# Second-layer modulation vectors: from TensorE steps to weighted sums on VectorE

## The chip, the core and the metric

The kernel runs on one core of one Trainium2 chip. The metric is the device time of one execution in microseconds. The kernel before takes 1640.04 us, the median of three runs (1639.86 to 1642.47).

## What is computed

Two blocks follow each other on 256 tokens of width 1024. The first block has two layers: a hybrid layer (sliding-window attention beside a chunked delta rule), then a recurrent one, each with a squared-ReLU MLP of hidden width 4096. The second block has two layers with two streams, the 256 tokens and 256 context tokens. Its layer 0 works on both streams; its layer 1, the last, needs of the context only keys and values, and its MLP has one stream. Each layer of the second block is steered by modulation vectors: for both of two conditioning vectors it needs six vectors of 1024,

```
m = silu(c) @ w_mod[i] + b_mod[i]        # c: (1024,), w_mod[i]: (1024, 6 * 1024)
shift1, scale1, gate1, shift2, scale2, gate2 = split(m, 6)
h  = rmsnorm(x, g) * (1 + scale1) + shift1
```

The two conditioning vectors (one for the tokens, one for the context) are known from the start, so the vectors of both layers can be computed at any time before they are used. The weights w_mod are 2 x 25 MB in fp32, of 259.77 MB that the kernel moves in all.

## The kernel before

**Numbers.** Large products run on TensorE as three products of fp32r pairs: each weight unit (1 MB, tile `wr`) is split by `w_split` (L395) into a high part `wh`, a cast on ScalarE (L407), and a rest `wl`, a difference on VectorE (L408). Four such pairs of 1024 columns are kept, two raw units. `w_next` (L424) loads the next unit and splits one half ahead.

**Order.** The program is written out as Python generators that are woven. At build time a planner orders the instructions of each engine: an instruction's rank is its place in the program, and of those whose inputs and buffers are there in the planner's own model the one of lowest rank goes first. `tc.high_priority(-10)` gives ranks ten places later. The engines then work through fixed orders, and an instruction that waits holds the ones behind it on its engine. So a step may run long before the place where it is written, where its engine has a pause, its tiles are there and a buffer is free; at its place it is due.

**The steps.** `mods` (L749) is a generator of 48 steps, 24 for each of the second block's layers i: three pairs q of vectors, eight pieces k of 128 rows each. A step needs two tiles `wm` of 128 x 1024 (512 KB each, four buffers, loaded by `mod_load`, L728). It makes four matmuls of the conditioning columns `cs_t[:, k]` (128 x 32) with 512 columns of weights each, into four bands of 32 output partitions of the bank `pm`, and sums over k there. After the eighth, bias and gain (`bg`) are applied on VectorE, the gates go to DRAM (`mdr`), and `cols_of` transposes shift and scale into the columns `mc`.

**Where the steps are written.** `fill(n)` takes n steps. 18 are in `some_mods` (L1204), woven with the delta rule and the attention of the hybrid layer, one in every second round; two after it (L1219); four in each MLP of one stream in the first block (L614) and two after the first of them (L1234); two after the recurrent layer (L1368); 2 + 2 + 4 in layer 0 of the second block (L1770, L1786, L1852); two near the end of the MLP of both streams (L1967); 2 + 1 + 1 and the rest in layer 1 (L1860 to L1899).

**The MLP of both streams,** `mlp512` (L1911): a w1 unit feeds `up` for both streams (2 x 48 matmuls of 256 columns into `pb`); a pair of w2 units feeds `acc` for four token tiles and two halves (96 matmuls of 512 columns into `pa`), whose results VectorE adds up (L1937). The order of the units is fixed by `_mlp_order_512`: three w1, then by turns a pair of w2 and two w1. Rows of gains and gates for other places use the tile `row` of three buffers (L444, L1371).

Of the kernel before, what the change touches and what calls it, by code (L numbers as in the profile page):

```python
# [10 lines left out]
F32 = mybir.dt.float32  # L11
# [4 lines left out]
P = 128  # L16
# [1 line left out]
SM = 1.0 / math.sqrt(96.0)  # L18
NW = 4
LEAD = 96  # L20
TRAIL = 24
ALPHA = 4.0 ** 0.25

ADD, SUB, MUL, MAX, MIN, POW = ALU.add, ALU.subtract, ALU.mult, ALU.max, ALU.min, ALU.pow
# [262 lines left out]
def _take(g, n):  # L287
    for _ in range(n):
        next(g, None)
# [4 lines left out]
def hybrid_then_mla(ctx: ExitStack, tc: tile.TileContext, a, out, usizes):  # L294
    nc = tc.nc
    V, S, G, T = nc.vector, nc.scalar, nc.gpsimd, nc.tensor
# [10 lines left out]
    def nm(s):  # L307
        uid[0] += 1
        return f"{s}_{uid[0]}"
# [4 lines left out]
    def s4(shape, dt=F32):  # L314
        return tmp.tile(shape, dt, tag="s4", bufs=5, name=nm("s4"))
# [19 lines left out]
    def psM():  # L335
        return psp.tile([P, 512], F32, tag="pm", bufs=1, name=nm("pm"))
# [4 lines left out]
    def mm(o, l, r, start, stop):  # L341
        T.matmul(o, l, r, start=start, stop=stop)  # L342
# [98 lines left out]
    half = cpool.tile([P, 8], F32, name="half")  # L441
    V.memset(half, -0.5)

    def row(name, n=1024, o=0):  # L444
        r = tmp.tile([P, 1024], F32, tag="row", bufs=3, name=nm("row"))
        i = ROWS.index(name)
        nc.sync.dma_start(out=r[:, :n], in_=a["rows"][i : i + 1, o : o + n].to_broadcast([P, n]))
        return r
# [274 lines left out]
        V.tensor_tensor(c2, c2, th, op=MUL)  # L723

    class WM:
        tiles, n = {}, 0

    def mod_load():  # L728

        if WM.n >= 48:  # L730
            return
        i, q, k = WM.n // 24, WM.n // 8 % 3, WM.n % 8
        for j in range(2):
            wm = wpool.tile([P, 2, 512], F32, tag="wm", bufs=4, name=nm("wm"))
            if WM.n < 2:
                G.tensor_copy(wm[:, 0, 0:1], WM.after)
            nc.sync.dma_start(out=wm, in_=a["wm"][i, q, k, j].rearrange("p (a b) -> p a b", a=2))
            WM.tiles[WM.n, j] = wm
        WM.n += 1

    mc = cpool.tile([P, 2, 3, 32], F32, name="mc")
    cpool.tile([P, TRAIL], F32, name="trail")

# [5 lines left out]
    def mods():  # L749

        def cols_of(m, i, q):
            pt = psC()
            for c in range(4):
                tr(pt[:, 128 * c : 128 * c + 128], m[:, 128 * c : 128 * c + 128])
            V.tensor_copy(mc[:, i, q].rearrange("p (c r s) -> p c r s", c=4, r=4),
                          pt.rearrange("p (c r s) -> p c r s", c=4, r=4)[:, :, :, 0:2])

        todo = None
        for n in range(48):
            i, q, k = n // 24, n // 8 % 3, n % 8  # L760
            if k == 0:
                ps = psM()
            if k == 1 and todo:
                cols_of(*todo)
            if k == 4:
                bg = s4([P, 2, 512])
                for r in range(4):
                    nc.sync.dma_start(
                        out=bg[32 * r : 32 * r + 32],
                        in_=a["bg"][i, q, r : r + 1].rearrange("o (a b) -> o a b", a=2).to_broadcast([32, 2, 512]),  # L770
                    )
            while WM.n < min(n + 2, 48):
                mod_load()
            for r in range(4):
                with tc.high_priority(-10):
                    mm(ps[32 * r : 32 * r + 32, :], cs_t[:, k, :], WM.tiles[n, r // 2][:, r % 2, :], k == 0, k == 7)
            mod_load()
            if k < 7:
                yield
                continue  # L780
            m = s2([P, 512])
            V.tensor_tensor(m, ps, bg[:, 0, :], op=ADD)
            V.scalar_tensor_tensor(m, m, K("one")[:, q : q + 1], bg[:, 1, :], op0=ADD, op1=MUL)
            for r in range(4):
                if 2 * q + r // 2 in (2, 5):
                    nc.sync.dma_start(
                        out=mdr[i, :, 2 * q + r // 2, 512 * (r % 2) : 512 * (r % 2) + 512], in_=m[32 * r : 32 * r + 2]
                    )
            todo = (m, i, q)
            yield  # L790
        cols_of(*todo)
        yield

    mod_g = mods()

    def fill(n):
        _take(mod_g, n)

    def run(g):
        for _ in g:  # L800
# [2 lines left out]
    def hybrid():  # L803
# [398 lines left out]
            yield from attention(1)  # L1202

        def some_mods():  # L1204
            for _ in range(18):
                next(mod_g, None)
                yield
                yield

        _weave(delta_b(), att(), some_mods())  # L1210

# [643 lines left out]
    def layer1(xs, Ts, late):  # L1855

        m = Mixer(1)
        m.Ts = Ts
        w = (w_next(8), w_next(8))
        fill(2)  # L1860
        run(conf_inputs(m, w, 0))
        cg = conf_conv(m)
        late(0)
        w = (w_next(4), w_next(4))
        x0, x1 = latents(m, 1, 0, w), latents(m, 1, 1, w)
        _take(x0, 2)
# [24 lines left out]
        mc = lambda t: merge_conv(m, 1, t, gbr, cgb)  # L1891
        ma = lambda t: merge_attn(m, 1, t, gbr)
        side = pipelined(mc(0), mc(1), ma(0))
        at = attend(m, 1, 1)
        _take(at, 2)
        _pace(at, side, 1)
        run(side)
        run(ma(1))
        fill(99)  # L1899
        GP = mrow(1, 0, 2)  # L1900
        nT = Late()

        def done(t, halves):
            post_norm(xs[1][t], halves, GP)
            y = normed(xs[1][t])
            nT.fn[t] = lambda: to_xT(y, t, nT.xT, mod=(1, 1, 4))

        tm1024(m.mT[1], done, nT, (2, 3, 0, 1))
        return nT

    def mlp512(Ts, xs, late):  # L1911
# [27 lines left out]
        for kind, j in _mlp_order_512():  # L1939
            if kind == "w1":  # L1940
# [19 lines left out]
                elif j > 1:  # L1960
                    w = w_next(8)
                    for s in (1, 0):
                        up(j, w, s)
                        if j == 2 and s:
                            hid_tr(1)
                    if j >= 14:
                        fill(1)  # L1967
            elif j < 7:
                for c in range(2):
                    w = w_next(4)  # L1970
                    for n in range(4):
                        acc(j, c, w, n)
                del hid[2 * j], hid[2 * j + 1]
            else:
                GP = [mrow(0, 1, 5), mrow(0, 0, 5)]
# [80 lines left out]
```

## Time and profile before

| | |
|---|---|
| median of three runs | 1640.04 us |
| the profiled execution: its own time | 1642.03 us |
| its span, first to last instruction | 1640.0 us |
| TensorE busy | 1577.9 us (96%) |
| VectorE busy | 1035.3 us (63%) |
| ScalarE busy | 738.9 us (45%) |
| GpSimd busy | 94.7 us (6%) |
| moved from and to HBM | 259.77 MB, 158 GB/s on average |
| mean granted TensorE clock | 0.988 of full speed |

Of the span, the hybrid layer takes up to about 200 us, its MLP up to 400, the recurrent layer up to 520, its MLP up to 715, layer 0 of the second block up to 967, the MLP of both streams up to 1281, layer 1 up to 1457 and the last MLP the rest. The profile has a chain of waits: the work that ended last, followed back step by step to what released it. Time of an engine that is not in this chain costs nothing as long as it stays out of it. PE is TensorE, DVE VectorE, ACT ScalarE, POOL GpSimd, SP the engine that issues the transfers.

### The profile page before, as it was taken

How to read it: one execution, taken by the hardware profiler on the slowest of the kernel's cores; microseconds unless marked ns; L12 is line 12 of the kernel's file. 1: busy time of each engine (PE TensorE's matmuls, PEld its weight loads, DVE VectorE, ACT ScalarE, POOL GpSimd, SP SyncE). 2: the span in 40 equal slices, each digit the busy share in tenths (PEclk: the TensorE clock that was granted, in tenths of full speed). 3: DMA queues.
4: the chain of work that ended last, by engine and by line, in shares of the span. 5: the costliest groups of instructions: out<-in, count | busy, mean ns of one | idle time of the engine just before them, and what ended most of it. 6: DMA issues, size and time to landing. Idle time of an engine off the chain costs nothing.

```text
span 1640.0 us, 24918 instructions
## 1 busy us (share of the span) xinstructions
PE 1577.9 (96%) x10182; PEld 1359.7 (83%) x10182; DVE 1035.3 (63%) x1619; ACT 738.9 (45%) x1252; POOL 94.7 (6%) x121
## 2 busy tenths in 40 slices
PE   8899999999979999999999999999999999989998
PEld 7676689887868999878877799999999788779997
DVE  7884565557777555768974763444444799775555
ACT  5542344434563544536454543222223466554443
POOL 0021000000000000001100100000000031000000
PEclk9999999999989999999999999999999999999999
DMA  8755476555645655462310342322222263145553
GB/s 308 289 197 176 158 270 206 204 197 213 247 167 180 219 180 188 174 229 100 129 52 27 106 146 97 103 87 94 103 83 98 80 212 130 50 144 205 180 184 125
DMA packets 46946, 259.77 MB, mean 158 GB/s; under 512 B 5600, under 2 KB 5856, under 8 KB 24304
## 3 DMA queue, kind: packets, MB, share of 16 engines
q1 hardware_dynamic: 46832, 258.18, 44.7%
q8 instruction: 80, 1.31, 0.3%
q14 instruction: 34, 0.28, 0.1%
HBM read 257.08 MB, written 1.08 MB: 157 GB/s over the span
## 4 chain that ended last, share of the span: by engine, by line
PE 80%; DVE 9%; ACT 5%; DMA 3%; issue 2%; POOL 1%; SPq 0%; POOLq 0%; DVEq 0%; ACTq 0%
PE pa L342 46%; PE pb L342 27%; PE pm L342 4%; PE pb L366 2%; DVE wl L408 2%; DMA wr<-in_wp_dram 1%; DMA wm<-in_wm_dram 1%; ACT wh L407 1%; PE pc L366 1%; ACT s L1378 1%; DVE s L1572 1%; POOL ti L1384 1%; ACT s L1641 0%; DVE s L644 0%; DVE xt L659 0%
## 5 line engine op out<-in xcount | busy, mean ns | idle before, releaser
L408 DVE TENSOR_TENSOR wl<-wr,wh 128x1024 fp32r<-128x1024 f32 (+2 forms) x366 | 443.9, 1217 | 300.2 <-ACT wh L407 293.7
L407 ACT CAST wh<-wr 128x1024 fp32r<-128x1024 f32 (+2 forms) x364 | 376.8, 1042 | 406.5 <-PE pa L342 196.5
L342 PE MATMUL pa<-wh,b 128*128 128x512 f32 (+3 forms) x1456 | 409.6, 364 | 11.3 <-ACT b L816 5.4
L342 PE MATMUL pb<-b,wh 128*128 128x256 f32 x2240 | 406.2, 283 | 0.0
L342 PEld LDWEIGHTS pb<-b,wh 128*128 128x128 f32 x2240 | 352.6, 192 | 7.2 <-issue 3.4
L342 PE MATMUL pb<-b,wl 128*128 128x256 f32 x1120 | 317.5, 283 | 0.0
L342 PEld LDWEIGHTS pa<-wh,b 128*128 128x128 f32 x1456 | 266.8, 195 | 53.8 <-ACT b L816 5.4
L342 PE MATMUL pa<-wl,b 128*128 128x512 f32 (+3 forms) x728 | 258.3, 364 | 10.6 <-DVE wl L408 10.5
L342 PE MATMUL pa<-wh,s 128*128 128x512 f32 x768 | 244.4, 391 | 0.0
L342 PEld LDWEIGHTS pb<-b,wl 128*128 128x128 f32 x1120 | 215.0, 192 | 1.7 <-issue 1.7
L342 PE MATMUL pa<-b,wh 128*128 128x256 f32 x1056 | 199.1, 289 | 3.1 <-ACT wh L407 2.3
L342 PEld LDWEIGHTS pa<-b,wh 128*128 128x128 f32 x1056 | 166.4, 194 | 15.5 <-ACT wh L407 3.6
L342 PEld LDWEIGHTS pa<-wl,b 128*128 128x128 f32 x728 | 141.5, 194 | 36.8 <-DVE wl L408 15.1
L342 PEld LDWEIGHTS pa<-wh,s 128*128 128x128 f32 x768 | 144.3, 188 | 29.0 <-DVE s L454 0.3
L342 PE MATMUL pa<-b,wl 128*128 128x256 f32 x528 | 149.9, 287 | 0.8 <-DVE wl L408 0.8
L342 PE MATMUL pa<-wl,s 128*128 128x512 f32 x384 | 150.4, 392 | 0.0
L342 PEld LDWEIGHTS pa<-b,wl 128*128 128x128 f32 x528 | 101.4, 193 | 6.6 <-DVE wl L408 3.0
L342 PE MATMUL pm<-wm,cs_t 128*32 128x512 f32 x384 | 82.0, 611 | 8.3 <-DMA wm<-in_wm_dram 8.2
L559 DVE TENSOR_TENSOR s<-s 128x512 f32<-128x512 f32 x80 | 54.9, 686 | 51.5 <-ACT s L557 51.5
L342 PEld LDWEIGHTS pa<-wl,s 128*128 128x128 f32 x384 | 72.3, 188 | 14.8 <-DVE wl L408 1.4
L1572 DVE SCALAR_TENSOR_TENSOR s<-cu,cols_sb,s 128x512 f32<-128x512 f32 (+1 forms) x120 | 70.5, 619 | 0.5
L366 PE MATMUL pb<-kc_sb,s 128*128 128x128 f32 x366 | 58.2, 283 | 11.6 <-POOL s L1475 3.2
(279 smaller groups left out, 1397.6 us busy)
## 6 DMA issues: line engine op xcount, KB each, us to landing
wr<-in_wp_dram SPq DMA_DIRECT2D x176, 1024.0 KB, 4.8
wm<-in_wm_dram SPq DMA_DIRECT2D x96, 512.0 KB, 4.5
row<-in_rows_dram SPq DMA_DIRECT2D x10, 512.0 KB, 6.8
wr<-in_wp_dram SPq DMA_DIRECT2D x4, 832.0 KB
s<-in_bg_dram SPq DMA_DIRECT2D x24, 128.0 KB, 5.3
row<-mdr SPq DMA_DIRECT2D x6, 512.0 KB, 3.4
wr<-in_wp_dram SPq DMA_DIRECT2D x4, 264.0 KB, 3.3
b<-in_xT_dram SPq DMA_DIRECT2D x4, 256.0 KB, 5.7
```

What stands on the lines that cost most here:

```text
L342: T.matmul(o, l, r, start=start, stop=stop)
L366: T.transpose(o, i, ident)
L407: S.copy(h[:, :n], r)
L408: V.tensor_tensor(l[:, :n], r, f(h[:, :n]), op=SUB)
L559: V.tensor_tensor(q, r, r, op=MUL)
L1378: S.activation(j, x, AF.Square, scale=scale, accum_out=o)
L1384: G.tensor_tensor(r, e, half[:, :1], op=POW)
L1572: V.scalar_tensor_tensor(ac, src, w(k), ac, op0=MUL, op1=ADD)
```

## The change

Layer 0 of the second block keeps its 24 steps on TensorE. For layer 1 each 128 x 1024 tile of weights is multiplied on VectorE by one column of the conditioning vector and added to a running sum, for both vectors: two instructions a tile, 96 in all. After eight tiles each of the two sums (a `row` tile each) is summed over its 128 partitions by TensorE, with a 128 x 32 tile `sel` of zeros and one column of ones: per group of eight tiles four matmuls of 512 columns, 24 in all, two into each band. The 48 tiles of 512 KB are loaded one at a time, three to four ahead.

The places change: `some_mods` takes eight steps, one in every fifth round. `fill` stops once the first layer's last column is written, which its calls reach at the second `fill(2)` of layer 0. The second layer's steps are taken by `fill1` in the MLP of both streams: after each `up` from the third w1 unit on, and after each second `acc` up to the seventh pair of w2 units, 56 calls for 51 steps. Bias and gain of the second layer are loaded where they are used, and the columns transposed right behind.

```diff
-TRAIL = 24
+TRAIL = 88
...
+    def row_tile():
+        return tmp.tile([P, 1024], F32, tag="row", bufs=3, name=nm("row"))
...
     class WM:
-        tiles, n = {}, 0
+        tiles, n, first = {}, 0, False
+        order = [(0, q, k, j) for q in range(3) for k in range(8) for j in range(2)]
+        order += [(1, q, k, j) for q in range(3) for j in range(2) for k in range(8)]
+
+    def mod_load(upto):
+
+        for n in range(WM.n, min(upto, len(WM.order))):
+            at = WM.order[n]
             wm = wpool.tile([P, 2, 512], F32, tag="wm", bufs=4, name=nm("wm"))
-            if WM.n < 2:
+            if n < 4:
                 G.tensor_copy(wm[:, 0, 0:1], WM.after)
...
+    sel = cpool.tile([P, 2, 32], F32, name="sel")
+    V.memset(sel, 0.0)
+    for s_ in range(2):
+        V.memset(sel[:, s_, s_ : s_ + 1], 1.0)
...
+        for n in range(24):
+            q, k = n // 8, n % 8
...
+            mod_load(2 * n + 4)
             for r in range(4):
                 with tc.high_priority(-10):
-                    mm(ps[32 * r : 32 * r + 32, :], cs_t[:, k, :], WM.tiles[n, r // 2][:, r % 2, :], k == 0, k == 7)
-            mod_load()
+                    mm(ps[32 * r : 32 * r + 32, :], cs_t[:, k, :], WM.tiles[0, q, k, r // 2][:, r % 2, :], k == 0, k == 7)
+            mod_load(2 * n + 6)
...
         cols_of(*todo)
-        yield
+        yield "first"
+
+        for q in range(3):
+            ps = psM()
+            for j in range(2):
+                acc = [row_tile() for _ in range(2)]
+                for k in range(8):
+                    n = 48 + 16 * q + 8 * j + k
+                    mod_load(n + 3)
+                    w = WM.tiles.pop((1, q, k, j)).rearrange("p a b -> p (a b)")
+                    for s_ in range(2):
+                        c = cs_t[:, k, s_ : s_ + 1]
+                        with tc.high_priority(-10):
+                            if k == 0:
+                                V.tensor_scalar(acc[s_], w, c, None, op0=MUL)
+                            else:
+                                V.scalar_tensor_tensor(acc[s_], w, c, acc[s_], op0=MUL, op1=ADD)
+                    mod_load(n + 4)
+                    yield
+                for r in (2 * j, 2 * j + 1):
+                    with tc.high_priority(-10):
+                        for s_ in range(2):
+                            mm(ps[32 * r : 32 * r + 32, :], sel[:, s_, :], acc[s_][:, 512 * (r % 2) : 512 * (r % 2) + 512], s_ == 0, s_ == 1)
+            cols_of(*biased(ps, gains(1, q), 1, q))
+            yield
...
     def fill(n):
-        _take(mod_g, n)
+
+        for _ in range(n):
+            if not WM.first:
+                WM.first = next(mod_g) == "first"
+
+    def fill1():
+
+        next(mod_g, None)
...
         def some_mods():
-            for _ in range(18):
+            for _ in range(8):
                 next(mod_g, None)
-                yield
-                yield
+                for _ in range(5):
+                    yield
...
-        fill(99)
+        assert next(mod_g, None) is None
...
                         up(j, w, s)
+                        fill1()
                         if j == 2 and s:
                             hid_tr(1)
-                    if j >= 14:
-                        fill(1)
...
                         acc(j, c, w, n)
+                        if n % 2:
+                            fill1()
```

`gains` and `biased` are the loads and the two VectorE instructions that the steps had before, as functions.

## Rows read from the trace of the kernel before

**Rows 1.** The page: engine totals, and the chain that ended last, by engine.

```profile
PE 1577.9 (96%) x10182; PEld 1359.7 (83%) x10182; DVE 1035.3 (63%) x1619; ACT 738.9 (45%) x1252; POOL 94.7 (6%) x121
...
PE 80%; DVE 9%; ACT 5%; DMA 3%; issue 2%; POOL 1%; SPq 0%; POOLq 0%; DVEq 0%; ACTq 0%
```

**Rows 2.** The page, costliest groups: the modulation steps (busy us, mean ns).

```profile
L342 PE MATMUL pm<-wm,cs_t 128*32 128x512 f32 x384 | 82.0, 611 | 8.3 <-DMA wm<-in_wm_dram 8.2
```

**Rows 3.** Stretches, steps' tile alone: length, PE (records), PEld, DVE, clock, DMA share, GB/s.

```profile
0.00:100.00 100.00, 7.72 (x40) 1.25 (x40) 0.00 (x0) 0.98 0.82 294
100.00:200.00 100.00, 25.08 (x104) 3.57 (x104) 1.38 (x2) 1.00 0.49 169
200.00:970.00 770.00, 40.94 (x192) 6.55 (x192) 2.06 (x3) 0.98 0.48 170
970.00:1300.00 330.00, 0.00 (x0) 0.00 (x0) 0.00 (x0) 1.00 0.28 96
1300.00:1440.00 140.00, 8.26 (x48) 1.31 (x48) 0.68 (x1) 0.99 0.38 133
```

**Rows 4.** The same view of whole engines: PE, PEld, DVE, ACT, POOL, clock, DMA.

```profile
970.00:1300.00 330.00, 329.99 (x2083) 300.32 (x2082) 148.69 (x185) 102.04 (x138) 2.51 (x4) 1.00 0.28 96
1300.00:1400.00 100.00, 95.71 (x686) 81.73 (x686) 93.38 (x188) 64.78 (x129) 17.86 (x24) 1.00 0.42 149
```

**Rows 5.** Chain in order of time, pieces of steps: start us, us, records.

```profile
328.04 0.97 PE pm L342 x2
...
329.33 0.99 PE pm L342 x6
...
408.30 0.99 PE pm L342 x8
...
957.35 1.83 PE pm L342 x10
```

**Rows 6.** Chain between 100 and 205 us, shares by line.

```profile
by line: PE pb L342 36.7%; PE pa L342 25.8%; PE pm L342 23.7%; PE pa L366 2.9%; PE pb L366 2.8%; ACT s L963 2.2%; PE pc L366 1.6%; POOL ti L460 1.0%; ACT s L1145 0.7%; DVE s L1062 0.7%; DVE s L1061 0.7%; issue 0.6%; DVE ti L459 0.2%; DVE ti
```

**Rows 7.** Timeline in the hybrid layer: start us, us, instruction.

```profile
133.91 1.90 PE L342 MATMUL pm<-wm,cs_t 128*32 128x512 f32 x10
...
135.13 0.56 ACT L1013 COPY s<-pb 128x512 f32<-128x512 f32 x1
...
135.74 1.16 PE L342 MATMUL pb<-b,s 128*128 128x128 f32 x8
```

**Rows 8.** Chain, pieces of steps in layer 0, first and last of four.

```profile
782.29 0.97 PE pm L342 x2
...
959.77 0.99 PE pm L342 x6
```

**Rows 9.** Chain, pieces of steps in layer 1, first and last of five.

```profile
1340.04 0.99 PE pm L342 x8
...
1356.44 0.99 PE pm L342 x6
```

**Rows 10.** VectorE groups by shape (count | busy us, mean ns).

```profile
L1572 DVE SCALAR_TENSOR_TENSOR s<-cu,cols_sb,s 128x512 f32<-128x512 f32 x60 | 43.3, 744 | 0.3
...
L1572 DVE SCALAR_TENSOR_TENSOR s<-cu,cols_sb,s 128x256 f32<-128x256 f32 x60 | 27.2, 494 | 0.2
...
L1397 DVE TENSOR_SCALAR s<-xt,ti 128x512 f32<-128x512 f32 x16 | 7.1, 484 | 4.2 <-POOL ti L1384 4.1
```

**Rows 11.** MLP of both streams: a split's difference; two pieces of the chain.

```profile
1058.45 1.23 DVE L408 TENSOR_TENSOR wl<-wr,wh 128x1024 fp32r<-128x1024 f32 x1 [0.23 <-ACT wh L407]
...
1045.89 23.03 PE pb L342 x192
1068.92 21.79 PE pa L342 x96
```

**Rows 12.** Timeline of TensorE in the recurrent layer.

```profile
437.04 1.92 PE L342 MATMUL pm<-wm,cs_t 128*32 128x512 f32 x2 [2.26 <-DMA wm<-in_wm_dram]
```

**Rows 13.** Timeline of SP: a load of a row tile.

```profile
923.78 0.34 SPq L1373 DMA_DIRECT2D row<-mdr  x1
```

More of the change, by code (lines that the diff above doesn't have):

```diff
@@ L725, in hybrid_then_mla @@
     class WM:
-        tiles, n = {}, 0
[L728 to L733, printed above, removed]
+        tiles, n, first = {}, 0, False
[4 more added lines that the diff above has]
+            at = WM.order[n]
             wm = wpool.tile([P, 2, 512], F32, tag="wm", bufs=4, name=nm("wm"))
-            if WM.n < 2:
+            if n < 4:
                 G.tensor_copy(wm[:, 0, 0:1], WM.after)
-            nc.sync.dma_start(out=wm, in_=a["wm"][i, q, k, j].rearrange("p (a b) -> p a b", a=2))
-            WM.tiles[WM.n, j] = wm
-        WM.n += 1
+            nc.sync.dma_start(out=wm, in_=a["wm"][at].rearrange("p (a b) -> p a b", a=2))
+            WM.tiles[at] = wm
+            WM.n = n + 1
+    sel = cpool.tile([P, 2, 32], F32, name="sel")
+    V.memset(sel, 0.0)
+    for s_ in range(2):
+        V.memset(sel[:, s_, s_ : s_ + 1], 1.0)
     mc = cpool.tile([P, 2, 3, 32], F32, name="mc")
@@ L756, in cols_of, with gains, biased @@
                           pt.rearrange("p (c r s) -> p c r s", c=4, r=4)[:, :, :, 0:2])
[L758 to L772, printed above, removed]
-                mod_load()
-            for r in range(4):
-                with tc.high_priority(-10):
-                    mm(ps[32 * r : 32 * r + 32, :], cs_t[:, k, :], WM.tiles[n, r // 2][:, r % 2, :], k == 0, k == 7)
-            mod_load()
-            if k < 7:
-                yield
-                continue
+        def gains(i, q):
+            bg = s4([P, 2, 512])
+            for r in range(4):
+                nc.sync.dma_start(
+                    out=bg[32 * r : 32 * r + 32],
+                    in_=a["bg"][i, q, r : r + 1].rearrange("o (a b) -> o a b", a=2).to_broadcast([32, 2, 512]),
+                )
+            return bg
+        def biased(ps, bg, i, q):
             m = s2([P, 512])
@@ L788, in mods @@
                     )
-            todo = (m, i, q)
+            return m, i, q
+        todo = None
+        for n in range(24):
+            q, k = n // 8, n % 8
+            if k == 0:
+                ps = psM()
+            if k == 1 and todo:
+                cols_of(*todo)
+            if k == 4:
+                bg = gains(0, q)
+            mod_load(2 * n + 4)
+            for r in range(4):
+                with tc.high_priority(-10):
+                    mm(ps[32 * r : 32 * r + 32, :], cs_t[:, k, :], WM.tiles[0, q, k, r // 2][:, r % 2, :], k == 0, k == 7)
+            mod_load(2 * n + 6)
+            if k < 7:
+                yield
+                continue
+            todo = biased(ps, bg, 0, q)
             yield
         cols_of(*todo)
-        yield
+        yield "first"
+        for q in range(3):
+            ps = psM()
+            for j in range(2):
[7 more added lines that the diff above has]
+                        with tc.high_priority(-10):
+                            if k == 0:
+                                V.tensor_scalar(acc[s_], w, c, None, op0=MUL)
[4 more added lines that the diff above has]
+                for r in (2 * j, 2 * j + 1):
+                    with tc.high_priority(-10):
+                        for s_ in range(2):
+                            mm(ps[32 * r : 32 * r + 32, :], sel[:, s_, :], acc[s_][:, 512 * (r % 2) : 512 * (r % 2) + 512], s_ == 0, s_ == 1)
+            cols_of(*biased(ps, gains(1, q), 1, q))
+            yield
     mod_g = mods()
     def fill(n):
-        _take(mod_g, n)
+        for _ in range(n):
[3 more added lines that the diff above has]
+        next(mod_g, None)
     def run(g):
@@ L1204, in some_mods @@
         def some_mods():
-            for _ in range(18):
+            for _ in range(8):
                 next(mod_g, None)
-                yield
-                yield
+                for _ in range(5):
+                    yield
         _weave(delta_b(), att(), some_mods())
```

## The prediction

> **What bounds the kernel now.** I read the engine totals first: TensorE is busy 96% of the span and holds 80% of the chain of waits [rows 1]. The reader should see that only work or waits on TensorE's path count. The costliest-groups part gives the steps that the change is about: 384 records, 82.0 us on TensorE [rows 2], two records a matmul, so 48 steps of eight records, 1.71 us a step on average. The table by stretch [rows 3] says where they ran: 5 steps before 100 us, 13 up to 200, 24 up to 970, none in the MLP of both streams (970 to 1300), 6 after it. Steps 40 and 41, written into that MLP (L1967), had thus run before it: the planner draws steps forward into TensorE's pauses. The same stretches for whole engines [rows 4]: in that MLP TensorE is busy 329.99 of 330 us, VectorE 148.7 of 330, DMA moves 96 GB/s; from 1300 to 1400 VectorE is busy 93%. So the change puts VectorE work where VectorE has room, and what is left of it for TensorE where TensorE has none.
>
> **What a step costs.** In the chain of waits a lone matmul of a step (2 records) takes 0.97 us, three (6 records) 0.99, all four 0.99, but five (10 records) 1.83 [rows 5]. Four matmuls into four bands of 32 output partitions run side by side; one into a band that is busy waits, 0.84 us more. A step whose matmuls are issued together costs 1.0 us; one that the planner cuts in two, as at 328 us between matmuls of one and the same weight unit, costs 0.97 + 0.99 = 1.96. A step in a pause costs nothing.
>
> **Part by part.**
> 1. *Weave in the hybrid layer: eight due steps instead of 18.* In 100 to 205 us the steps hold 23.7% of the chain [rows 6], 24.9 us, 1.91 for each of 13. Ten go. Ends: 0, if each sat in a pause, and 19.1, if none did. Both kinds are there: at 133.91 ten records end at 135.8, but the product behind them needed a ScalarE copy that ran from 135.13 to 135.69 [rows 7], a pause whatever TensorE does; others stand ahead of products whose inputs were ready. I take half of the chain price, about 1.03 a step: **-10.3**. The transfers go along: ten steps are 20 tiles of 512 KB fewer on SP's queue in this stage; at nothing, as no wait on a weight unit ends the chain between 100 and 205. What is late next is the chain of 128x128 products and their copies.
> 2. *200 to 970: 16 steps instead of 24.* The places up to the recurrent layer keep one step each, first-layer ones now, at the same price. What falls away is the last eight: in the chain four pieces from 782.29 to 959.77 [rows 8], together 0.97 + 1.84 + 1.83 + 0.99 = 5.6. Ends 0 and -5.6. I take the two at 957 and 959 (2.8) whole, since TensorE works without a pause around them, and the two near 782 (2.8) half, since VectorE is loaded there: **-4.2**.
> 3. *1300 to 1440: six steps go.* Five pieces in the chain, 1340.04 to 1356.44 [rows 9], 4.9 us. VectorE at 93% is close behind there, so half: **-2.5**, ends 0 and -4.9. The stage's weight-column loads leave SP's queue too: three stand directly ahead of a weight unit's; at nothing.
> 4. *The sums on TensorE: 24 matmuls, six groups of four, in the MLP.* Each group writes two bands, twice each, in the order band, same band, next band, same band. By rows 5 the second waits for the first, the third runs beside the second, the fourth waits: 0.99 + 0.84 + 0.84 = 2.67, six times **+16.0**, with no pause to hide in. Ends: 11.0, if a group takes the time of two matmuls (6 x 1.83), and 23.3, if all are cut apart (24 x 0.97). I take the middle value since the pieces of rows 5 that are cut are cut once.
> 5. *The sums on VectorE.* No such instruction of 1024 columns is in the trace. The tap instruction takes 494 ns at 256 columns and 744 at 512 [rows 10], so 1.244 us at 1024 by the same slope, and the first of each sum (tensor_scalar, 484 ns at 512) at most 0.97. 84 x 1.244 + 12 x 0.97 = 116 us. In a steady cycle of 23.03 + 21.79 = 44.8 us (four weight units) [rows 11] VectorE works 45% [rows 4], 20 us; eight steps add 16 x 1.24 = 19.9: 89% full. Cover: the weight split. Its cast starts when TensorE frees the buffer, the second difference of a unit starts at 1058.45, is done at 1059.7, and TensorE takes up that unit at 1068.92 at the earliest [rows 11]: 9 us. A sum ahead of it costs 1.24 of these. So **0**, upper end +15 (below). Bias and column transposes are three per layer before and after: 0. Of what is queued behind a sum that waits for its tile: splits, the MLP's additions and its squares, all on VectorE's one queue.
> 6. *Transfers in the MLP.* 48 tiles of 0.52 MB are 25 MB in 314 us, 80 GB/s on top of 96; the first 100 us moved 294 [rows 3]. SP's order takes them between weight units; the weight buffer has the cover of point 5. **0**.
> 7. *Constants.* Three small VectorE writes at the start, while the first weights land: 0. They and the larger pad move no other work.
>
> Sum: -10.3 - 4.2 - 2.5 + 16.0 = -1.0. The profiled execution took 1642.03 (span 1640.0), 2.0 above the runs' median of 1640.04; so 1641.0 in a profile, **1639.0** as a median. The point: four matmuls that ran as one are replaced by four of which three queue, in the one stage without a pause. Own range of this case, with half the ends of points 1 and 4: 1632 to 1646.
>
> **A rule beside it.** In rows 5 the fifth matmul waits for the first, its band. The Trainium skill, TensorEngine Tiling (Array Packing), section Key Properties, says that different tiles execute loads and matmuls in parallel, each independently. If that holds whatever the order of issue, the two bands of a group run side by side and point 4 would be 11.0, not 16.0; by issue in order it is 16.0. The rows above show no two matmuls of a band directly behind each other, so they don't decide it.
>
> **Rivals.**
> - *Pauses are kept, the work isn't the bound (slower).* The planner already puts steps where TensorE would wait, and the removed ones were that filler; the hybrid's products and copies set its time. For: the piece of rows 7, and 200 to 970 where steps vanish into pauses. Against: 23.7% of the chain. Then points 1 to 3 give 2.0, 2.8 and 0, the sums cost 16.0 all the same: +11.2, 1651. It decides as soon as less than 0.9 of the 1.91 us of a hybrid step is really waited for.
> - *The chain price is right (faster).* 19.1 + 5.6 + 4.9 - 16.0 = 13.6 less, 1626. For: TensorE's chain there has hardly a gap. Against: rows 7.
> - *Bands overlap* as above: -6.0, 1634.
> - *VectorE's queue in the MLP (slower).* A sum that waits for its tile holds a split behind it. TensorE waited 2.26 us for such a tile at 437 [rows 12]; six groups at 2.5 each make +15 - 1, 1654. It decides where a delay passes 9 us. Against: four tiles are in flight.
> - *The sums don't run in the MLP.* They share three row buffers, and now the planner loads rows for later into them long ahead, one at 923.78 for the end of the MLP [rows 13]. If two are taken so, the sums wait for the MLP's end, and the first third, 32 instructions of 1.24, stands ahead of the next layer: +39, 1678. Against: the sums have the lower rank.
>
> **How the numbers follow.** Forecast case 0.47, pauses 0.15, chain price 0.22, bands 0.05, VectorE's queue 0.07, row buffers 0.04. A change of 0.2%, 3.3 us, is about what can be told from none. The forecast case gives faster 0.14, same 0.27, slower 0.06; chain price and bands are faster (0.27), the other three slower (0.26): 0.41, 0.27, 0.32. The range 1624 to 1654 takes in all but the row-buffer case, half of VectorE's queue, the far ends of the chain price and of sums cut apart.
>
> **What would show it.** Right: in the changed profile about 2.7 us of TensorE per group of sums inside the MLP, that MLP longer by some 16 us with TensorE still full, VectorE near 80% there; the hybrid stage shorter by about 10; the stretch after the MLP by 2 or 3. Wrong: groups at 1.8 or 3.9; TensorE idle in the MLP, released by a VectorE difference (point 5); a hybrid stage of the same length (point 1) or shorter by 19; sums later than 1280 us. A change beyond 15 us either way would mean that a stage I costed at nothing moved.

## The result, and the profile after

The changed kernel takes **1651.5 us** in the median (1649.0 to 1653.2), the kernel before 1640.05 (1639.9 to 1642.5): ratio **1.0059**, 95% interval 1.0042 to 1.0077. It is slower. Forecast was 1639.0, about no change. (The quotient of the two medians, four runs each, is 1.0070, inside the interval. In 80 more runs beside the experiments the kernel before had medians of 1642.5 to 1643.4.)

First the page of the changed kernel: engine totals, the chain that ended last by engine, and the group of the new sums.

```profile
PE 1561.4 (95%) x10038; PEld 1355.4 (82%) x10038; DVE 1141.5 (69%) x1718; ACT 739.1 (45%) x1252; POOL 97.2 (6%) x121
...
PE 76%; DVE 10%; ACT 5%; POOL 2%; issue 2%; DMA 1%; POOLq 0%; DVEq 0%; ACTq 0%
...
L821 DVE SCALAR_TENSOR_TENSOR row<-wm,cs_t,row 128x1024 f32<-128x1024 f32 x84 | 106.0, 1280 | 1.8 <-DMA wm<-in_wm_dram 1.3
```

TensorE lost 16.5 us of work against [rows 1], VectorE gained 106 us, and yet the span went from 1640.0 to 1646.9. So TensorE has more idle time than before, and some of the work left is dearer. The tile of the steps by stretch, as in [rows 3] (columns: length, PE, PEld, DVE, clock, DMA share, GB/s):

```profile
0.00:100.00 100.00, 6.99 (x40) 1.24 (x40) 0.00 (x0) 1.00 0.79 289
100.00:200.00 100.00, 11.39 (x50) 1.69 (x50) 0.68 (x1) 1.00 0.30 103
200.00:970.00 770.00, 23.46 (x102) 3.38 (x102) 1.36 (x2) 0.98 0.45 159
970.00:1300.00 330.00, 16.22 (x48) 2.56 (x48) 2.06 (x3) 1.00 0.46 157
```

Next, the same pieces of the chain of waits in both kernels (start, length, what): the first MLP's steady beat, the last product ahead of layer 0, layer 0's second run of products, the start and the end of the MLP of both streams, and the last MLP. The start of the MLP of both streams is marked by its first long run of products into `pa`, 12.5 us behind the 967 us at which it begins. Before:

```profile
223.32 5.76 PE pb L342 x48
...
688.01 11.22 PE pa L342 x48
...
726.69 11.61 PE pa L342 x95
...
979.51 20.65 PE pa L342 x91
...
1281.61 5.47 PE pa L342 x24
...
1465.07 5.76 PE pb L342 x48
```

After:

```profile
205.72 5.76 PE pb L342 x48
...
670.70 11.23 PE pa L342 x48
...
715.17 11.68 PE pa L342 x95
...
968.08 21.56 PE pa L342 x95
...
1289.42 5.48 PE pa L342 x24
...
1471.94 5.76 PE pb L342 x48
```

Subtract line by line: -17.6, -17.3, -11.5, -11.4, +7.8, +6.9. The hybrid part gave **17.6** back. Layer 0's start lost **5.8** of them. The MLP of both streams, 302.1 us long before and 321.3 now, took **19.2**. Layer 1 gave 0.9. That is the whole of the +6.9 in the two traces.

The medians differ by 11.4. The kernel before took 1642.03 in its profiled execution, 2.0 above its median. The changed kernel took 1649.0 in its own, 2.5 below its median; that was its fastest, at a mean granted clock of 0.989, and its three others, 1651.2 to 1653.2, had 0.984 to 0.986. These three have no trace. The profiles of the experiments show one place where an execution can lose as much: from the end of the MLP of both streams to the last MLP it is 182.5 us in the changed kernel and 182.7 in early_q, but 186.4 to 186.8 in sum_per_q, uncut, few_sums, early_q_gate and weave2, whose edits touch no instruction there. So 4 us between two profiled spans are not by themselves a difference of the programs. The profiled execution of wl_early ran late in its span at a granted clock far below all others (0.455 in the mean) and is read up to 961 us only, where the clock was 0.99 in every stage.

**Layer 0's start.** In the kernel before, the stretch from 688.00 to 726.70 us holds five steps, 40 records, and TensorE is busy 38.43 of its 38.70 us. In the changed kernel no step is left there, and TensorE waits 12 of 44.5 us. The steps' tile in the kernel before:

```profile
688.00:726.70 38.70, 7.82 (x40) 1.43 (x40) 0.00 (x0) 1.00 0.62 214
```

The timeline of TensorE in the changed kernel, and two stretches of all engines (length, PE, PEld, DVE, ACT, POOL, clock, DMA share, GB/s):

```profile
698.37 0.58 PE L342 MATMUL pa<-b,wl 128*128 128x256 f32 x1 [7.17 <-DVE wl L408]
```

```profile
691.00:698.40 7.40, 0.23 (x3) 0.03 (x1) 7.24 (x17) 3.44 (x8) 0.92 (x1) 0.63 0.13 40
698.40:703.00 4.60, 4.60 (x21) 4.60 (x22) 3.74 (x5) 0.00 (x0) 1.40 (x1) 0.50 0.83 261
```

TensorE waits 7.17 us for the low part of a weight unit and then works 4.6 us at a granted clock of 0.50, the lower of its two levels (1.2 GHz). VectorE was busy 7.24 of the 7.40 us: with what, its own timeline says.

```profile
695.11 0.74 DVE L670 SCALAR_TENSOR_TENSOR xt<-xt,ti,row 128x512 f32<-128x512 f32 x1
695.77 1.41 DVE L672 SCALAR_TENSOR_TENSOR xt<-xt,ti,row 128x512 f32<-128x512 f32 x2
697.10 1.22 DVE L408 TENSOR_TENSOR wl<-wr,wh 128x1024 fp32r<-128x1024 f32 x1
```

The split stands last, behind the normalization of the x stream. In the kernel before it came ahead of those instructions, and steps lay around it. Its VectorE and its TensorE at that place:

```profile
708.22 1.21 DVE L408 TENSOR_TENSOR wl<-wr,wh 128x1024 fp32r<-128x1024 f32 x1
```

```profile
705.90 1.90 PE L342 MATMUL pm<-wm,cs_t 128*32 128x512 f32 x10
...
708.76 1.06 PE L342 MATMUL pm<-wm,cs_t 128*32 128x512 f32 x6
709.75 0.39 PE L342 MATMUL pa<-b,wl 128*128 128x256 f32 x1
```

**The MLP of both streams.** Its sums' matmuls in the chain: one group in three pieces, one uncut (two records a matmul, four matmuls a group); then the whole stage.

```profile
1007.99 0.97 PE pm L342 x2
...
1009.28 0.98 PE pm L342 x4
...
1010.58 0.98 PE pm L342 x2
...
1157.81 1.85 PE pm L342 x8
```

```profile
970.00:1290.00 320.00, 320.00 (x1975) 278.55 (x1974) 220.88 (x241) 90.55 (x113) 0.00 (x0) 1.00 0.47 158
```

TensorE is busy without a gap, as before [rows 4], VectorE 69%. Four of the six groups are cut (2.8 to 2.9 us), two are whole (1.85). Of the 96 sums on VectorE 78 lie in this stage; 18 lie in layer 0, from 881 us on.

### The profile page after: what moved, and what is told of

Its sections match the earlier page's. It is cut to its first block, busy times and chain, and to the rows that moved or that the text cites. A ratio compares the mean times of both kernels' runs of the same rounds, so it can differ in the third digit from the quotient of the medians.

```text
span 1646.9 us, 24742 instructions
## 1 busy us (share of the span) xinstructions
PE 1561.4 (95%) x10038; PEld 1355.4 (82%) x10038; DVE 1141.5 (69%) x1718; ACT 739.1 (45%) x1252; POOL 97.2 (6%) x121
## 4 chain that ended last, share of the span: by engine, by line
PE 76%; DVE 10%; ACT 5%; POOL 2%; issue 2%; DMA 1%; POOLq 0%; DVEq 0%; ACTq 0%
PE pa L342 43%; PE pb L342 27%; PE pm L342 3%; PE pb L366 2%; DVE wl L408 1%; DVE s L1616 1%; ACT wh L407 1%; PE pc L366 1%; POOL ti L1428 1%; DMA wm<-in_wm_dram 1%; DVE s L647 1%; ACT s L1422 1%; ACT s L1685 0%; DVE s L1441 0%; DMA wr<-in_wp_dram 0%
## 5 line engine op out<-in xcount | busy, mean ns | idle before, releaser
L821 DVE SCALAR_TENSOR_TENSOR row<-wm,cs_t,row 128x1024 f32<-128x1024 f32 x84 | 106.0, 1280 | 1.8 <-DMA wm<-in_wm_dram 1.3
```

Of the source, the lines that this page charges most:

```text
L821: V.scalar_tensor_tensor(acc[s_], w, c, acc[s_], op0=MUL, op1=ADD)
```

## The experiments

Stages are read from each profile at the marks above: weave end (first steady beat of the first MLP), layer 0 (from the start of the last product ahead of it, 670.70 in the changed kernel, to the start of the MLP of both streams), and that MLP. wl_early is read up to that MLP only.

| kernel | weave end | layer 0 | MLP, both streams | ratio to before, 95% |
|---|---|---|---|---|
| before | 223.3 | 291.5 | 302.1 | |
| changed | 205.7 | 297.4 | 321.3 | 1.0059 (1.0042-1.0077) |
| pe_steps | 208.9 | 299.5 | 341.2 | 1.0192 (1.0176-1.0208) |
| weave18 | 222.8 | 298.2 | 321.3 | 1.0152 (1.0130-1.0174) |
| wl_early | 206.3 | 289.0 | | 1.0000 (0.9990-1.0010) |
| sum_per_q | 206.1 | 301.3 | 309.6 | 0.9999 (0.9986-1.0012) |
| uncut | 206.5 | 298.7 | 315.7 | 1.0022 (1.0006-1.0038) |
| few_sums | 205.5 | 298.2 | 317.0 | 1.0007 (0.9997-1.0018) |
| before_early | 223.3 | 292.1 | 302.1 | 1.0008 (0.9996-1.0020) |
| early_q | 206.7 | 294.5 | 309.6 | 0.9955 (0.9942-0.9967) |
| early_q_gate | 205.9 | 293.3 | 309.4 | 0.9940 (0.9927-0.9954) |
| hold_q | 209.1 | 320.5 | 309.6 | 1.0041 (1.0027-1.0055) |
| weave2 | 206.3 | 289.9 | 309.4 | 0.9947 (0.9925-0.9968) |
| weave2_later | 205.6 | 289.7 | 309.4 | 0.9998 (0.9987-1.0010) |

Some 3 us of layer 0 can come from the execution alone: early_q_gate and weave2 differ in the weave only and had 293.3 and 289.9 there, and over 3 of these 3.4 us lie between 671 and 846 us, at a granted clock of 0.97 and 0.99.

### What the MLP pays for

**pe_steps**: the second layer as TensorE steps at the new places.

```diff
-                            V.scalar_tensor_tensor(acc[s_], w, c, acc[s_], op0=MUL, op1=ADD)
...
-                            mm(ps[32 * r : 32 * r + 32, :], sel[:, s_, :], acc[s_][...], s_ == 0, s_ == 1)
+                    mm(ps[32 * r : 32 * r + 32, :], cs_t[:, k, :], WM.tiles[1, q, k, r // 2][:, r % 2, :], k == 0, k == 7)
```

> The changed kernel with the second layer's vectors again as 24 steps of four matmuls on TensorE, at the places that the change gives them (mostly the MLP of both streams), no sums on VectorE. Theory (in that stage TensorE is the bound, and what a step costs is its own time there): 24 x 0.97 (uncut) to 24 x 1.96 (cut in two by other matmuls) = 23 to 47 us in the stage in place of the 16.2 us of the sums' matmuls, so a span 7 to 31 us above the changed kernel's 1646.9, near 1654 to 1678. Rival (VectorE's 96 sums are what lengthens the stage, by holding back the evictions): the stage is no longer than with the sums, and the span stays at or under 1647.

Measured: span 1674.4, the stage 39.1 us longer than before with 16 of the 24 steps in it. Each is cut the same way, as this pair of pieces of its chain shows:

```profile
1058.01 0.97 PE pm L342 x2
...
1059.30 0.99 PE pm L342 x6
```

So a step in a stage without a pause costs 1.96 and about 0.4 more for the neighbours of the cut (39.1 less 16 x 1.96 and three column transposes of 0.44, over 16). The sums on VectorE are the cheaper form, by 27.5 us of span, or 1.3% (22 us) by the ratios. The theory held, its rival fell.

**sum_per_q**: one group of eight in place of two of four, five row buffers.

```diff
-                for r in (2 * j, 2 * j + 1):
-                    with tc.high_priority(-10):
-                        for s_ in range(2):
-                            mm(..., sel[:, s_, :], acc[s_][...], s_ == 0, s_ == 1)
+            for s_ in range(2):
+                for r in range(4):
+                    mm(..., sel[:, s_, :], accs[r // 2][s_][...], s_ == 0, s_ == 1)
```

> The changed kernel with all eight sum matmuls of a third of the vector together (the four sums of it held in five row buffers in place of three), at the rank of the other matmuls, no longer four and four at a lowered rank. Theory (groups of four are cut by other matmuls and cost 2.8 us where cut and 1.85 uncut; bands run side by side, so eight matmuls in four bands cost what four in two bands do): three groups of 1.85 = 5.6 us in place of 16.2, the MLP of both streams 10 to 11 us shorter, span near 1636.5, ratio to before about 0.9995. Rival 1 (bands do not overlap beyond two): 3 x 3.7 = 11 us, span near 1642. Rival 2 (the VectorE work lengthens the stage, not the matmuls): span within 2 us of 1646.9.

One of its three pieces in the stage's chain:

```profile
1154.36 1.85 PE pm L342 x16
```

Eight matmuls in four bands, two of a band, cost 1.85 us, no more than four in two bands. The stage fell to 309.6 us, 11.7 less. The span fell only to 1643.7: layer 0 had grown by 3.9 us, which nobody had forecast. The chain there shows why: five row buffers let the planner start the sums earlier, and they stand in the attention's chain.

```profile
860.03 1.19 DVE row L822
...
861.83 1.19 DVE row L822
863.16 1.54 POOL ti L463
```

From the first to the last of the six small GpSimd instructions of L463 in that chain it is 34.9 us, against 30.6 in the changed kernel. Another 3.8 us were lost behind the MLP, where the spread between executions lies.

**uncut**: groups of four, three row buffers, but at the matmuls' own rank.

```diff
-                for r in (2 * j, 2 * j + 1):
-                    with tc.high_priority(-10):
-                        for s_ in range(2):
+                for s_ in range(2):
+                    for r in (2 * j, 2 * j + 1):
```

> The changed kernel, with each group of four sum matmuls at the rank of the other matmuls and ordered so that neighbours write different bands; three row buffers and six groups as before. Theory (four of six groups were cut by other matmuls, and a cut group costs about 1 us more since its bands no longer run side by side): six groups of 1.85 us = 11.1 in place of 16.2, the MLP of both streams 316 us in place of 321.3, 5 us less in all: span near 1642. Rival (what mattered in the run with all eight together was only the number of groups; a cut costs nothing): within 1.5 us of 321.3.

Measured: 315.7 us for the stage, six pieces of 1.84 us (the first below), 5.6 us less than with the cuts, as the theory had it. The span moved by 0.8 the other way, 1647.7 at a clock of 0.982, for this execution took 4.1 us more behind the MLP and 1.3 more in layer 0; by the ratios it is 0.4% faster than the changed kernel, with intervals that just part.

```profile
1009.20 1.84 PE pm L342 x8
```

**few_sums**: 72 of the 96 sums left out.

```diff
-                            else:
+                            elif k == 7:
                                 V.scalar_tensor_tensor(acc[s_], w, c, acc[s_], op0=MUL, op1=ADD)
```

> The changed kernel with the sums over slices 1 to 6 left out (24 of the 96 VectorE instructions stay, the weight blocks are still loaded, the 24 sum matmuls stay); so the second layer's vectors miss those six slices. Theory (in the MLP of both streams TensorE is busy 100% and VectorE's sums hide behind it): that stage stays within 1 us of 321.3 us; what goes is at most the few sums that lie before it, in the end of layer 0, under 3 us: span 1644 to 1647. Rival (the sums on VectorE hold back evictions or weight splits in the stage): it gets 5 us or more shorter and the span falls to 1642 or less.

The stage is 4.3 us shorter, between the two bounds, so the run decides by its rows only: the sums' matmuls in it are 38 records with 12.2 us in place of 48 with 16.2, since one group now lies before the stage. That is 4.0 of the 4.3. The sums on VectorE themselves cost TensorE nothing there. By the ratio this kernel is 0.5% faster than the changed one; its profiled span of 1645.9 is only 1.0 lower, since this execution took 4.0 us more behind the MLP. That leaves some 4 of the 0.5% (8 us) that no trace explains.

### Layer 0's start

**wl_early**, and **before_early**, the same edit in the kernel before:

```diff
-        w = (w_next(8), w_next(8))
+        w = (w_next(8, 100), w_next(8))
         run(conf_inputs(m, w, 0))
```

> The changed kernel, with the first weight split of layer 0 ranked 100 places earlier, so that VectorE makes it ahead of the end of the MLP's normalization instead of behind it. Theory (TensorE's 7.2 us idle at 691 us and the half clock after it come from VectorE's order alone, and there is no step left to fill it): the idle shrinks below 2 us, no half clock follows, layer 0 starts 4 to 6 us earlier and the end moves with it: span 1641 to 1643, ratio to before about 1.002. Rival (the wait moves on to the x stream's transposed input, which the same normalization makes): the idle turns up within 20 us on another tile and the span stays within 1.5 us of 1646.9.

> The kernel before, with only the first weight split of layer 0 ranked 100 places earlier. Theory (the kernel before had the split ahead and steps to fill with; the changed kernel lost both): nothing to gain here but the steps' own time, within 2 us of the kernel before, layer 0's second stretch at 726 to 728 us. Rival (the static order is worth the same in both kernels, whatever the change did): 5 to 8 us faster, ratio 0.995 to 0.997.

wl_early comes out at 1.0000, 0.6% under the changed kernel, 9.7 us: more than the 4 to 6 forecast. Its trace has 8.4 of them in layer 0, all ahead of the second run of products, which the changed kernel starts at 715.17:

```profile
706.72 13.77 PE pa L342 x95
```

TensorE's waits ahead of it fall from 12 us to 4.8, the longest now 2.1 for another instruction of VectorE. Two points of the theory failed: the idle time did not go below 2 us, and a stretch at a lower clock still follows (0.54 over 706.7 to 712 us). The kernel before gains nothing (1.0008). So the order of VectorE is worth something only where the change has spoilt it and taken the filling steps away.

**early_q** has this edit and sum_per_q's.

> Both edits at once: the first weight split of layer 0 earlier, and the eight sum matmuls of a third together. By the stages of the single runs: the early split brought layer 0's second stretch from 715.2 to 706.7 us (8 us), the matmuls together took the MLP of both streams from 321.3 to 309.6 us, and gave 4 us back in layer 0, where more sums now lie. Theory (they touch different stages and add): span 1643.7 - 8 = 1635 to 1636, ratio to before about 0.995. Rival (the second wait eats the first's gain, for VectorE's order shifts again): span 1640 or more.

Measured: span 1630.8, ratio 0.9955, as the theory had it (the span is 4 us lower still, with the short layer 1); against sum_per_q's 0.9999 it is 7.2 us, and 6.8 of layer 0. Its VectorE has three splits ahead of the normalization's last instructions, and of TensorE's waits between 670 and 725 us (in all, times, longest) the one for a split is 0.4 us long in place of 7.2:

```profile
683.46 3.49 DVE L408 TENSOR_TENSOR wl<-wr,wh 128x1024 fp32r<-128x1024 f32 x3
686.87 1.41 DVE L672 SCALAR_TENSOR_TENSOR xt<-xt,ti,row 128x512 f32<-128x512 f32 x2
```

```profile
PE pb L366 <- DVE s L1442: 2.8, 1, 2.8
PE pa L342 <- ACT b L650: 1.5, 1, 1.5
PE pa L342 <- DVE wl L408: 0.4, 1, 0.4
```

Behind the wait of 2.8 us, at 701.95, the granted clock falls all the same (all engines):

```profile
702.00:708.00 6.00, 4.51 (x20) 4.12 (x21) 5.78 (x12) 2.05 (x4) 0.00 (x0) 0.50 0.00 1
```

**hold_q**: sum_per_q with the first layer's steps kept for layer 0.

```diff
-            if i % 3 == 1:
-                fill(1)
...
-        fill(2)
+        fill(6)
         late.ready(0)
...
-        fill(2)
+        fill(7)
         wq, wk = w_next(2, 100), w_next(1)
```

> sum_per_q with ten of the first layer's steps placed later: none in the MLPs and behind the first, six at the start of layer 0, seven before its queries. Theory (what is missing at the start of layer 0 is work that fills the wait for the weight split, as before): TensorE's 7.2 us idle at 691 us is filled, no half clock, and the steps cost nothing where they stood in the way at 300 to 500 us: 4 to 9 us less than sum_per_q's 1643.7 span, 1635 to 1640. Rival (a step costs its own time wherever it stands, and VectorE's order keeps the wait): span within 2 us of 1643.7.

A miss for both: slower than sum_per_q by 0.4%, layer 0 19 us longer. Its wait for the split is the same, and 13 us of steps went elsewhere, to a stretch at 740 us (waits of TensorE, then the steps' tile by stretch):

```profile
PE pa L342 <- DVE wl L408: 7.2, 1, 7.2
```

```profile
740.00:780.00 40.00, 13.09 (x46) 1.87 (x46) 0.69 (x1) 0.91 0.61 198
```

Steps at hand do not by themselves fill a wait: the planner puts them where its own plan has a pause. What helped was the order of VectorE.

### The sums ahead of their stage

**early_q_gate**: the loads for the sums wait for the MLP's first head.

```diff
+            elif 48 <= n < 52:
+                G.tensor_copy(wm[:, 0, 0:1], WM.gate)
...
-            mod_load(2 * n + 4)
+            mod_load(min(2 * n + 4, 48))
...
-            mod_load(2 * n + 6)
+            mod_load(min(2 * n + 6, 48))
...
                         before = n
+                    WM.gate = q[1][:, 0:1]
```

> As early_q, and the loads of the second layer's weight blocks held back until the MLP's first head is squared, so that no sum on VectorE lies before that stage. Theory (sums drawn into the end of layer 0 stand ahead of its last normalization on VectorE: with five row buffers that stretch took 3.9 us longer than in the changed kernel): layer 0 gets those 4 us back, the MLP stage stays at 309 to 311 us: span 1631 to 1633. Rival (the sums there lie in idle time; the 3.9 us came from the order of something else): span within 1.5 us of early_q's. A miss is also that the later sums push the last sum matmuls to the MLP's end: then the stage grows by 1 to 5 us.

Ratio 0.9940 against 0.9955, medians 1633.9 and 1637.1: 3 us, where 4 were expected; the intervals overlap. The MLP did not grow (309.4). The profiled execution, 1636.4 at a clock of 0.983, was the slowest of six; the others had spans of 1629.2 to 1633.4. What the gate gives back lies in layer 0's attention, not in its last normalization as the theory had it. From the first to the last of the six GpSimd instructions of L463 it is 35.0 us in early_q, 31.6 here and 30.6 in the changed kernel. All engines there, early_q and then early_q_gate:

```profile
840.90:875.90 35.00, 30.21 (x202) 22.61 (x200) 30.35 (x50) 15.72 (x41) 6.39 (x7) 0.95 0.32 96
```

```profile
846.10:877.70 31.60, 29.54 (x200) 22.62 (x199) 18.25 (x37) 15.90 (x41) 3.47 (x7) 0.95 0.01 1
```

From there to the mark of the MLP it is 87.1 us here, with no sum ahead of 959.73, 87.7 in early_q and 86.7 in wl_early with sums: the sums in that part cost nothing that shows. A GpSimd instruction of 128 x 1 elements in that part takes longer beside a VectorE split. First the changed kernel, VectorE and GpSimd,

```profile
924.08 1.22 DVE L408 TENSOR_TENSOR wl<-wr,wh 128x1024 fp32r<-128x1024 f32 x1
924.30 1.40 POOL L1428 TENSOR_TENSOR ti<-ti,half 128x1 f32<-128x1 f32 x1 [5.98 <-DVE ti L1427]
```

then one of the same line in early_q_gate, where VectorE has nothing to do meanwhile:

```profile
913.46 0.55 POOL L1431 TENSOR_TENSOR ti<-ti,half 128x1 f32<-128x1 f32 x1 [3.15 <-DVE ti L1430]
```

### What a step in the weave costs

**weave18**: the changed kernel with the old weave.

```diff
-            for _ in range(8):
+            for _ in range(18):
                 next(mod_g, None)
-                for _ in range(5):
+                for _ in range(2):
```

> The changed kernel with 18 first-layer steps in the hybrid part and two pauses after each, as before; all else as changed. Theory (each step there is on the path and also cuts into a chain that VectorE and ScalarE pace): the first MLP starts 17.6 us later again (223.3 in place of 205.7 us), and the ten steps no longer lie in the recurrent block and the MLPs around it, where they cost at most 10 x 0.97 = 9.7 us: span 1646.9 + 8 to 17.6, 1655 to 1664. Rival (the 17.6 us came from something else in the static order than the steps): the first MLP starts within 3 us of 205.7, span 1637 to 1650.

Measured: weave end 222.8, span 1662.5, within the theory's bounds. The 17.6 us are the ten steps. The steps' tile from 100 us to the weave's end, before and then after:

```profile
100.00:223.30 123.30, 31.19 (x130) 4.53 (x130) 1.38 (x2) 1.00 0.52 184
```

```profile
100.00:205.70 105.70, 11.39 (x50) 1.69 (x50) 0.68 (x1) 1.00 0.33 115
```

80 records and 19.8 us of TensorE went, and 17.6 us of time: 1.76 a step. That is the whole price in the chain: between 100 and 205 us the chain's pieces of steps hold 24.86 us over 113 records, 1.76 for every eight.

**weave2** and **weave2_later**: early_q_gate with two steps in the weave, the others right behind it, or in the MLPs.

```diff
-            for _ in range(8):
+            for _ in range(2):
                 next(mod_g, None)
...
-        fill(2)
+        fill(8)
```

```diff
-            for _ in range(8):
+            for _ in range(2):
                 next(mod_g, None)
...
             if i % 3 == 1:
-                fill(1)
+                fill(2)
```

> early_q_gate with two first-layer steps in the hybrid's weave in place of eight, and the six others right behind the hybrid's product. Theory (each step in the weave costs 1.76 us, as the ten that the change took out: 17.6 us over ten, in proportion): the weave ends 10.6 us earlier, the six steps cost 5.9 (0.98 each) or, where they fill a wait, less: first MLP 4 to 10 us earlier than 205.9, span 1626 to 1632. Rival (it was the overlong part only: the first eight lie beside idle time of a chain that VectorE and ScalarE pace, and cost nothing): the weave ends no earlier, the six come on top, first MLP at 208 to 212, span 1638 to 1642.

> early_q_gate with two steps in the hybrid's weave and two, not one, at each of the four places in the MLPs; in the static order no step is left between the hybrid's last chains and the first MLP (with the six right behind the hybrid's product, the order had put them back into that part). In early_q_gate those four steps hold about 7 us of the chain before the first MLP. Theory (a step on that stretch costs its chain price, 1.8 us): the first MLP starts 6 to 8 us earlier than 205.9, near 199; the steps land in the first MLP at 0.98 to 1.96 each, 4 to 8 us: end within 3 us of early_q_gate, span 1630 to 1637. Rival (they fill pauses there and cost nothing): the first MLP starts where it did, within 2 us, and ends 4 to 8 us later: span 1638 to 1645.

weave2 tells nothing of the weave: the planner drew the steps back to where they had been, 50 records between 100 and 200 us as before the edit. In weave2_later they stay away, and the weave ends at 205.6 all the same, while TensorE's busy time in it falls (all engines; first early_q_gate, then weave2_later):

```profile
100.00:205.90 105.90, 101.45 (x689) 79.18 (x688) 68.63 (x119) 39.00 (x109) 18.69 (x16) 1.00 0.33 122
```

```profile
100.00:205.60 105.60, 97.98 (x668) 80.49 (x667) 67.84 (x117) 38.88 (x109) 18.86 (x16) 0.98 0.26 91
```

The rival held: the steps that the change had left there were free, although they held about as much of the chain as those taken out, 1.7 us each (10.67 us over 50 records in early_q_gate). From 180 us to the weave's end TensorE is busy without a gap in early_q_gate, with 26 records of steps; in weave2_later it waits 3.0 us there, 1.8 of them for a split. In the MLPs the steps were not free: the kernel is 0.6% slower than early_q_gate, and the last product ahead of layer 0 starts 8.3 us later. So the price of a step in the weave is not one number. Some lie in pauses of a chain that other engines pace; those beyond cost their whole price in the chain, and the chain alone does not tell the two apart.

## Why the prediction was wrong

- **Point 1**, the weave at -10.3: right in sign, mis-sized. It took half the chain price for all ten steps, since one row showed a step in a pause. weave18 and weave2_later show that the pauses were there, but that the steps which the change kept fill them; the ten it took were the dear ones, -17.6. Its chain price of 1.91 was also misread: [rows 6] goes on to 205 us, where the chain holds 113 records, 14 steps and not 13, so 1.76 a step and an end of 17.6, which is what came.
- **Point 2**, 200 to 970 us at -4.2: this is the step that failed. It counted the eight steps that fall away and priced them by four pieces of the chain from 782.29 us on; measured is +6.2 over 223.3 to 979.5 (756.2 before, 762.4 after). It put layer 0's start at nothing and did not ask what the steps there covered: five of them, 7.82 us, stood around a split, and with the program re-placed VectorE's order put that split last. The wait of 7.17 us and the half clock behind it make the start 5.8 us longer. wl_early and early_q take the wait away by order alone, before_early gains nothing from it. The rest of layer 0, where the four pieces lay, came out at +0.1 (252.8 us before, 252.9 after); why nothing was gained there stays open.
- **Point 3**, the stretch after the MLP at -2.5: measured -0.9, inside its ends.
- **Point 4**, the sums' matmuls at +16.0: measured +19.2 for the stage, of which 16.2 are the matmuls, 1.3 three column transposes of 0.44 us, and the rest, as far as can be told, the neighbours of the cuts; the point had counted neither of these there. That 16.2 stands so near 16.0 is luck: uncut groups cost 1.85, not 2.67, and four of six were cut, where the working had all uncut.
- **The bands**, the rival given 0.05: the two bands of a group run side by side in both orders of issue that were run: 1.85 us for a whole group of the changed kernel (band, same band, next band, same band), 1.84 in uncut, where neighbours write different bands. The Trainium skill, TensorEngine Tiling (Array Packing), section Key Properties, has different tiles work in parallel, each independently. The traces agree: 1.85 us for four matmuls in two bands (the changed kernel) and for eight in four (sum_per_q).
- **Point 5**, VectorE's sums at nothing: right in the MLP (TensorE 320.00 of 320 us busy; 1280 ns each against 1244 estimated). Not considered was that the planner starts them in layer 0. In the changed kernel that is from 881 us on, 18 of the 96, and costs nothing that shows; with five row buffers it is from 855 us on and costs 4.3 us in the attention.
- **The rivals**: "pauses are kept" gave 1651, the time measured, by another way: it had the weave at -2.0 and nothing lost in layer 0. "The chain price is right" was right on the weave alone. The range, 1624 to 1654, holds the result. The forecast case's own range, by half the ends of points 1 and 4, adds up to 1632 to 1648, not 1646, and does not hold it.

Of the four points the first missed by -7.3, the second by +10.4, the third by +1.6 and the fourth by +3.2: +7.9 together, from the forecast -1.0 to the +6.9 of the traces. That the sum is off by less than its second term is luck, for the first missed the other way. The 4.5 us by which the medians differ beyond the traces go with the granted clock; layer 1 is one place where profiled executions differ by as much, and whether the changed kernel's other runs lost them there stays open.

A version better than both came out of the runs: early_q_gate, the change with its sum matmuls in three groups of eight, the first split of layer 0 ranked earlier and the sums' loads held to their stage, at 0.9940 (0.9927 to 0.9954).

## What to carry to other kernels

Price a removed filler by what it filled: the ones beyond the pauses are worth their whole time, the ones inside nothing, and a wait that was covered comes out when they go. The chain of waits shows both kinds with the same price. After moving work, look at the order of the engine that feeds the bound one, since a planner re-ranks more than what was moved. Small matmuls into separate bands belong together and uncut.

## What the runs showed of the hardware

- Eight matmuls into four bands, two of a band, take 1.85 us together (sum_per_q); each piece that other matmuls cut off takes 0.97 to 0.98 alone, one with two matmuls of the same band 1.84 (the changed kernel).
- A wait of 7.17 us of TensorE was followed by 4.6 us at a granted clock of 0.50; in early_q a wait of 2.8 us was followed by 6 us at 0.50, in which TensorE waited another 1.5.
- A GpSimd instruction of 128x1 takes 0.55 us where VectorE is idle (early_q_gate, 913.46) and 1.40 beside a VectorE difference of 1.22 us that had begun 0.2 us before it (the changed kernel, 924.30). The Trainium skill, SBUF — State Buffer, section SBUF: two separate sides, has VectorE instructions with two SBUF inputs and GpSimd's exclude each other on a shared pair of ports. The trace agrees with that (0.55 and 1.40); no run here isolates it.
